# The gated convolution's input projection by seven block products, and block products added up in PSUM

## The chip, the cores and the metric

The kernel runs on one core of a Trainium2 chip. The metric is the device time of one execution in microseconds. Of several executions the median is given, with the lowest and the highest. PE is the matmul engine, PEld its weight loads, DVE the vector engine, ACT the scalar (activation) engine, POOL the general one, SP the engine whose queue issues most transfers. PSUM is the memory into which PE writes; it has eight banks of 512 float32 values per partition.

## The reference

The program takes 1024 prompt tokens and 32 sample tokens through two layers of width 1024. Layer 0 has one input projection of 2048 columns: 512 for a pooling mixer (trailing means over 2, 4, 8 and 16 tokens, by groups of 128 channels) and 3 x 512 for a gated short convolution. Cut to that part:

```python
hcat = x @ w_in_even                            # (tokens, 2048)
a_in, b_gate, c_gate, h_in = hcat[..., :512], hcat[..., 512:1024], hcat[..., 1024:1536], hcat[..., 1536:]
ya = pool_mixer(a_in)                           # trailing means minus the token, a map per group
cv = w[0]*ch[t-2] + w[1]*ch[t-1] + w[2]*ch[t]   # ch = c_gate * h_in, causal, three taps
yb = b_gate * cv
mix = concat(ya, yb) @ w_out_even
x = LN(alpha * x + mix)
x = LN(alpha * x + (silu(x @ w1) * (x @ w3)) @ w2)   # SwiGLU, 2816 hidden features
x = x + (ple @ w_ple) * sigmoid(x @ w_gate)
```

Layer 1 has other mixers (spatial gating, a state-space scan) and the same output projection, SwiGLU and embedding. All matrices are float32, and the result has to keep that precision.

## The kernel before, in words

Activations lie on chip with features on partitions: `xh` and `xl` are the operand of all 1056 tokens in two float32r parts whose sum is exact, `stream` is the residual. A weight is loaded (`Weights.raw`, L76), split into two parts in the same way (`Weights.split`, L86: the high part on ACT, the low part on DVE) and kept in a ring of four places of two halves each (`place`, `half`, L63 to L74). `plan` (L147) writes down the order of use; `get` (L135) hands a weight out and prepares those that follow, four halves ahead. A product of weight and operand takes three matmuls: high by high, low by high, high by low.

**Layer 0's mixer** (`layer0_mixer`, L317). The four pooling tiles come first, two at a time (windows 2 and 4, then 8 and 16). `feature_mm` (L232) makes one output tile of 128 features for one chunk of tokens (384, 384, 288): 8 k-tiles by 3 matmuls. ACT copies it out (L352 to L355); DVE makes the window sums (L361) and differences (L368 to L374); a small product maps each group (L380). Then the convolution: four groups of three tiles (c_gate, h_in, b_gate), for each chunk three `feature_mm`, a copy of c_gate on ACT (L392), the product c_gate * h_in (L396), the three taps (L399, L401), and the gate (L407). The results go to `yf`, which is split into the operand of the output projection (L414). PSUM holds six banks "mm" and two "ms".

**The up projection of SwiGLU** (`up`, L829) makes hidden tiles two at a time by Winograd's form of Strassen's algorithm: with the contraction and the pair of tiles cut in halves, and the tokens in halves of 528, seven products of blocks replace eight. `block_sums` (L878) makes the sums T1 to T4 of the operand's blocks, each in two parts. One product (L902) is 4 k-tiles by 3 by two matmuls of 264 columns, 24 in all, into a PSUM tile of two banks; "q" has four such tiles. `quad` (L934) takes the seven products of a pair in the order 1, 6, 7, 5, 2, 3, 4, each in a PSUM tile of its own; one is copied to SBUF by ACT (L937), and DVE adds the others there, seven additions (L922). Then come silu on ACT (L930) or the multiplication with silu's result on DVE (L932). There are nine such rounds of two pairs (w1, w3) in each layer, behind a first pair in an order of its own. During the last pair the first loads of the down projection go out (`load`, L1039), each behind the product that is the last to read the memory they overwrite.

The order of the instructions of each engine is fixed when the program is built: from those whose operands are ready by its own reckoning the builder takes the one that stands first in the program, so an instruction can come ahead of earlier ones that still wait. A tile of memory is handed out again when all its readers are done; a new pool's tiles wait for those of closed pools whose memory they take. On the chip each engine takes its queue in that fixed order.

```python
def quad(self, key, dst, gate, last=False):                    # L934
    nc.scalar.activation(self.block(dst, 0, 0), self.product(key, 1), AF.Copy)
    self.add(dst, (0, 1), self.product(key, 6), (0, 0))
    ...
    self.add(dst, (1, 0), self.product(key, 4))
    self.act(dst, gate)
```

Of the kernel before, what the change touches and what calls it, by code (L numbers as in the profile page):

```python
# [14 lines left out]
P = 128  # L15
# [16 lines left out]
# Matmul time, in us, from a chunk's last product to its statistics' matmuls, on to their broadcast, and  # L32
# between the pieces of what is normalised.
# [17 lines left out]


class Weights:
    """What the matmuls take beside the operand kept on chip, in the order of its use: loaded, then split
    exactly, w = hi + lo, into two float32r parts, AHEAD half places ahead of the matmuls."""
# [3 lines left out]
    def __init__(self, nc, pool, order):  # L59
        self.nc, self.pool, self.count, self.rest = nc, pool, 0, None  # L60
        self.made, self.items, self.temps = [], self._make(order), None
# [20 lines left out]
    def temp(self, n):  # L82
        self.count += 1
        return self.temps.tile([P, TH], F32, tag="bf", name=f"bf{self.count}", bufs=5)[:, :n]
# [12 lines left out]
    def _make(self, order):  # L97
        for kind, key, src in order:
# [7 lines left out]
            else:  # L106
                # The blocks of two hidden tiles' weights, and Winograd's sums of them.
                r0, r1 = (self.raw(v) for v in src)
                a11, a12, a21, a22 = (r[:, h * 512:(h + 1) * 512] for r in (r0, r1) for h in range(2))
                own = lambda x: (key, 1, self.split(self.half(), x))  # noqa: E731  # L110
                if kind != "sums":
                    yield own(a11)
                if kind == "own":
# [3 lines left out]
                if kind != "own":  # L117
                    yield own(s2)
                    yield own(self.sub(a11, a21))
                    yield own(s1)  # L120
                if kind == "all":
                    yield own(a12)
                if kind != "sums":
                    yield own(self.sub(a12, s2))
                if kind == "all":
                    yield own(a22)
# [20 lines left out]
def plan(a, steps, ple):  # L147
    """The order in which the weights are used."""
# [6 lines left out]
    for layer in range(2):  # L155
        if layer == 0:
            add("w_in0", *range(16))
# [24 lines left out]
class Later(list):  # L182
    """Chunks of an operand, whose last pieces may be still to come from deferred steps."""
# [11 lines left out]
class Kernel:  # L195
# [16 lines left out]
    def passed(self, columns):  # L212
        """Account for matmul columns issued; run the steps that are due."""
# [5 lines left out]
    def mm3(self, ps, w, sel, x, k, lo, n, first, last):  # L219
        """ps += W_k^T x_k with both operands in two exact parts."""  # L220
# [11 lines left out]
    def feature_mm(self, w, x, c, kk=KD, sel=None, k0=0):  # L232
        """One output tile [128 features, tokens of chunk c]."""
# [12 lines left out]
    def build(self):  # L246
        nc, tc, a = self.nc, self.tc, self.a
        with ExitStack() as ctx:
# [7 lines left out]
            self.stream = const.tile([P, KD, T], F32, name="stream")  # L256
            self.acc = [self.stream[:, :, t0:t0 + n] for t0, n in CH]
# [4 lines left out]
            nc.sync.dma_start(out=self.acc[0][:, 0:2, :], in_=xin[:, 0:2, t0:t0 + n])  # L262
            self.w.prefetch()
            for c, (t0, n) in enumerate(CH):
                for k in range(0 if c else 2, KD, 2):
                    nc.sync.dma_start(out=self.acc[c][:, k:k + 2, :], in_=xin[:, k:k + 2, t0:t0 + n])
# [16 lines left out]
            for c in range(3):  # L283
                for k in range(0, KD, 2):
                    self.split(self.x[c], slice(k, k + 2), self.acc[c][:, k:k + 2, :])
# [3 lines left out]
            # The hidden tiles, [parity, token half, pair, tokens of the half].  # L289
            self.hidden = [dram.tile([P, 2, 2, NG, TH], F32, name=f"hidden{i}") for i in range(2)]  # L290
            for layer in range(2):
                (self.layer1_mixer if layer else self.layer0_mixer)(self.x)
                with ExitStack() as stack:
                    self.hp = stack.enter_context(tc.tile_pool(name=f"h{layer}", bufs=1, reuse_waits="tile"))
                    self.w.temps = self.hp
# [14 lines left out]
    def split(self, x, ks, src):  # L310
        """x = hi + lo, exactly, for k-tiles ks of some tokens."""
# [5 lines left out]
    def layer0_mixer(self, x):  # L317
        nc, tc, a = self.nc, self.tc, self.a
        W = 15 + SEQ + 15 + DEC
        with ExitStack() as ctx:  # L320
            mp = ctx.enter_context(tc.tile_pool(name="mix0", bufs=1, reuse_waits="tile"))
# [3 lines left out]
            self.psum_bufs = {"mm": 6, "ms": 2}  # L325
# [4 lines left out]
            yf = [mp.tile([P, KD, CH[c][1]], F32, tag=f"yf{c}", name=f"yf{c}") for c in range(3)]  # L330

            # Products of zeros bring the tensor engine's clock up while the first loads come.
            zeros = yf[0][:, 0, :]
            nc.vector.memset(zeros, 0.0)
            ps = self.bank("ms")
            for _ in range(WARM):
                nc.tensor.matmul(ps[:, :CH[0][1]], zeros[:, :P], zeros, start=True, stop=True)

            ds = []
            for g0 in (0, 2):  # L340
                units = self.w.get(("w_in0", g0), ("w_in0", g0 + 1))
                us = []
# [1170 lines left out]
```

## Time and profile before

| what | value |
|---|---|
| three runs | 2346.04, 2354.27, 2354.75 us; median 2354.27 |
| profiled execution | span 2343.1 us from its first to its last instruction; no time besides its span is listed |
| mean granted clock of PE | 0.998 of 2.4 GHz |
| PE busy | 2322.3 us, 99% of the span |
| DVE busy | 1580.9 us, 67% |
| ACT busy | 905.2 us, 39% |
| moved by DMA | 203 MB, 87 GB/s on average |

Busy time of PE counts pipelined matmuls, so its durations (0.28 us for a matmul of 264 columns) overlap; the distance between the starts of two matmuls is what one costs. A wait is put down to the instruction that ended last before it. The stages lie like this: pooling to 58.5 us, the convolution to 202 us, output projection, norm and the first two hidden tiles to some 350 us, the up projection from there to 762 us, the down projection behind it; layer 1 fills the second half.

### The profile page before, as it was taken

How to read it: one execution, taken by the hardware profiler on the slowest of the kernel's cores; microseconds unless marked ns; L12 is line 12 of the kernel's file. 1: busy time of each engine (PE TensorE's matmuls, PEld its weight loads, DVE VectorE, ACT ScalarE, POOL GpSimd, SP SyncE). 2: the span in 40 equal slices, each digit the busy share in tenths (PEclk: the TensorE clock that was granted, in tenths of full speed). 3: DMA queues.
4: the chain of work that ended last, by engine and by line, in shares of the span. 5: the costliest groups of instructions: out<-in, count | busy, mean ns of one | idle time of the engine just before them, and what ended most of it. 6: DMA issues, size and time to landing. Idle time of an engine off the chain costs nothing.

```text
span 2343.1 us, 40948 instructions
## 1 busy us (share of the span) xinstructions
PE 2322.3 (99%) x17423; PEld 2289.4 (98%) x17423; DVE 1580.9 (67%) x2494; ACT 905.2 (39%) x1501; POOL 71.2 (3%) x88
## 2 busy tenths in 40 slices
PE   9999999999999999999999999999999999999998
PEld 8999999999999999999999989999999999999998
DVE  4434698666666878776655774788666665978773
ACT  4212254323232443464542662354232222434462
POOL 0000010000000000010000120100000000000100
PEclk9999999999999999999999999999999999999999
DMA  4110113222224622024211322122222225611132
GB/s 156 47 55 28 42 59 110 73 92 73 79 82 137 247 78 69 28 82 140 88 47 40 109 64 79 37 73 101 79 84 67 88 68 199 227 60 47 40 100 92
DMA packets 81289, 203.03 MB, mean 87 GB/s; under 512 B 10220, under 2 KB 16564, under 8 KB 81108
## 3 DMA queue, kind: packets, MB, share of 16 engines
q1 hardware_dynamic: 80340, 199.74, 25.8%
q8 instruction: 137, 2.24, 0.4%
q10 hardware_dynamic: 768, 0.68, 0.1%
q14 instruction: 44, 0.36, 0.0%
HBM read 167.24 MB, written 33.16 MB: 86 GB/s over the span
## 4 chain that ended last, share of the span: by engine, by line
PE 93%; DVE 3%; DMA 1%; POOL 1%; ACT 1%; issue 0%; SPq 0%; POOLq 0%; ACTq 0%
PE q L910 32%; PE q L1108 20%; PE mm L224 8%; PE mm L225 8%; PE mm L226 8%; PE q L1236 8%; PE q L1215 2%; PE mm L568 1%; PE mm L569 1%; PE mm L570 1%; DVE bf L94 1%; DMA raw<-w 1%; PE ms L704 1%; DVE w L89 0%; PE q L1317 0%
## 5 line engine op out<-in xcount | busy, mean ns | idle before, releaser
L1108 PE MATMUL q<-w 128*128 128x264 f32 x3696 | 458.3, 286 | 0.0
L1108 PEld LDWEIGHTS q<-w 128*128 128x128 f32 x3696 | 457.3, 189 | 0.0
L88 ACT ACTIVATE w<-raw 128x512 fp32r<-128x512 f32 (+2 forms) x240 | 189.6, 799 | 288.8 <-PE mm L226 107.6
L89 DVE TENSOR_TENSOR w<-raw,w 128x512 fp32r<-128x512 f32 (+2 forms) x240 | 218.3, 911 | 56.9 <-ACT w L88 56.1
L88 ACT ACTIVATE w<-bf 128x512 fp32r<-128x512 f32 (+1 forms) x226 | 138.3, 631 | 303.0 <-PE q L910 132.6
L224 PE MATMUL mm<-xhin,w 128*128 128x384 f32 (+1 forms) x672 | 219.2, 327 | 2.6 <-ACT w L88 1.5
L226 PE MATMUL mm<-xlin,w 128*128 128x384 f32 (+1 forms) x672 | 217.4, 325 | 0.0
L225 PE MATMUL mm<-xhin,w 128*128 128x384 f32 (+1 forms) x672 | 217.1, 324 | 0.0
L910 PE MATMUL q<-xhgate,w 128*128 128x264 f32 x1280 | 207.9, 284 | 1.4 <-ACT xhgate L884 0.8
L910 PE MATMUL q<-xhin,w 128*128 128x264 f32 x1280 | 208.0, 284 | 0.7 <-DVE c L815 0.6
L224 PE MATMUL mm<-xhgate,w 128*128 128x384 f32 (+1 forms) x576 | 188.2, 327 | 1.1 <-ACT xhgate L313 1.1
L226 PE MATMUL mm<-xlgate,w 128*128 128x384 f32 (+1 forms) x576 | 186.7, 325 | 0.0
L225 PE MATMUL mm<-xhgate,w 128*128 128x384 f32 (+1 forms) x576 | 186.6, 325 | 0.0
L910 PEld LDWEIGHTS q<-xhgate,w 128*128 128x128 f32 x1280 | 177.0, 188 | 1.8 <-ACT xhgate L884 1.0
L910 PEld LDWEIGHTS q<-xhin,w 128*128 128x128 f32 x1280 | 177.0, 188 | 1.1 <-issue 0.8
L89 DVE TENSOR_TENSOR w<-bf,w 128x512 fp32r<-128x512 f32 (+1 forms) x226 | 152.0, 690 | 23.4 <-ACT w L88 22.2
L1236 PE MATMUL q<-xhgate,w 128*128 128x264 f32 x1024 | 166.7, 285 | 0.0
L922 DVE TENSOR_TENSOR c<-c,q 128x528 f32<-128x528 f32 x142 | 98.0, 702 | 99.5 <-PE q L910 99.4
L922 DVE TENSOR_TENSOR s<-s,q 128x528 f32<-128x528 f32 x142 | 97.7, 701 | 78.5 <-PE q L910 78.1
L1236 PEld LDWEIGHTS q<-xhgate,w 128*128 128x128 f32 x1024 | 141.6, 188 | 0.0
L224 PEld LDWEIGHTS mm<-xhin,w 128*128 128x128 f32 x672 | 126.4, 188 | 4.7 <-ACT w L88 2.3
L910 PE MATMUL q<-xlgate,w 128*128 128x264 f32 x640 | 130.0, 284 | 0.4 <-DVE xlgate L885 0.4
(301 smaller groups left out, 4286.8 us busy)
## 6 DMA issues: line engine op xcount, KB each, us to landing
raw<-w SPq DMA_DIRECT2D x116, 512.0 KB, 3.6
hidden<-c SPq DMA_DIRECT2D x44, 528.0 KB, 3.9
raw<-w_gate SPq DMA_DIRECT2D x32, 512.0 KB, 3.6
raw<-w_in SPq DMA_DIRECT2D x16, 512.0 KB, 3.6
raw<-w_out SPq DMA_DIRECT2D x16, 512.0 KB, 3.6
xhdown<-hidden SPq DMA_DIRECT2D x12, 528.0 KB, 9.0
t2down<-hidden SPq DMA_DIRECT2D x8, 528.0 KB, 3.9
t3down<-hidden SPq DMA_DIRECT2D x8, 528.0 KB, 4.9
```

The source lines that it names most:

```text
L88: self.nc.scalar.activation(hi, x, AF.Copy)
L89: self.nc.vector.tensor_tensor(lo, x, hi.bitcast(F32), op=ALU.subtract)
L94: self.nc.vector.tensor_tensor(t, a, b, op=op)
L224: nc.tensor.matmul(ps, wh, xh, start=first, stop=False)
L225: nc.tensor.matmul(ps, wl, xh, start=False, stop=False)
L226: nc.tensor.matmul(ps, wh, xl, start=False, stop=last)
L568: nc.tensor.matmul(o, xh, hi[:, s], start=k == 0, stop=False)
L910: nc.tensor.matmul(ps[:, a, :TH // 2], w[q][:, ks], x[r][:, k, a * TH // 2:(a + 1) * TH // 2], start=k == 0 and j == 0, stop=k == 3 and j ...
L922: self.nc.vector.tensor_tensor(self.block(dst, *at), self.block(dst, *(to or at)), ps, op=ALU.add)
L1108: nc.tensor.matmul(ps[m][:, a, :TH // 2], v[q][:, ms], x[r][:, a * TH // 2:(a + 1) * TH // 2], start=j == 0 and n == 0, stop=j == NG - 1 a ...
L1215: nc.tensor.matmul(ps[:, b, :TH // 2], w[q][:, o:o + P], pe[k][r][:, t * TH + b * TH // 2:t * TH + (b + 1) * TH // 2], start=k == 0 and i ...
L1236: nc.tensor.matmul(ps[:, b, :TH // 2], w[q][:, ks], token_half((self.xh, self.xl), k, t, b)[r], start=k == 0 and i == 0, stop=k == KD - 1 ...
```

## The change

The twelve tiles of the convolution are made in six pairs by the seven products (c_gate, h_in and b_gate of tiles 0 and 1, then of 2 and 3). For this the mixer makes T1, T2, T3 from the raw input in the pooling stage, and T4 at the start of the convolution, over part of the operand. T1 and T2 lie in the memory of `stream`, so the raw input goes to a tile of the mixer instead, and the residual is loaded again during and behind the last pair (`residual`). The pooling groups change places: windows 8 and 16 first. The taps run over all 1056 tokens at once.

`quad` takes the products in the order 1, 2, 6, 5, 7, 3, 4, in both layers' up projection too. Products 6, 7 and 4 are added by PE to the PSUM tile of product 1, product 3 to that of product 5; between them ACT copies the running sum to the blocks where it belongs, and DVE adds only products that are wanted elsewhere. `plan` and `_make` follow that order. The rest of the diff takes comments away.

```diff
-            add("w_in0", *range(16))
+            add("w_in0", 2, 3, 0, 1)
+            for i in (0, 2):
+                for j in range(3):
+                    order.append(("all", ("conv", j, i), [a["w_in0"][4 + 3 * (i + k) + j] for k in range(2)]))
...
+        xraw = self.mp.tile([P, KD, T], F32, tag="yf", name="xraw")
...
+    def residual(self, c):
+        t0, n = CH[c]
+        self.nc.sync.dma_start(out=self.acc[c], in_=self.a["xT"][:, :, t0:t0 + n])
...
+            self.psum_bufs = {"ms": 2, "mm": 6, "q": 3}
+            self.w.temps, self.w.temp_bufs = mp, 3
+            t3 = mp.tile([P, 8, TH], F32R, name="t3mix")
+            t12 = self.const.tile([P, 16, TH], F32R, tag="stream", name="t12mix", bufs=1)
...
+    def pooling(self, stack, x, xraw, wg, pool_out, sums):
+        pp = stack.enter_context(tc.tile_pool(name="pooling", bufs=1, reuse_waits="tile"))
...
+        for g0 in (2, 0):
+            units = self.w.get(("w_in0", g0), ("w_in0", g0 + 1))
+            if yf is None:
+                self.block_sums(xraw, *sums)
...
+    def gated_conv(self, stack, conv_out, t2, t4, b21):
+        cp = stack.enter_context(tc.tile_pool(name="conv0", bufs=1, reuse_waits="tile"))
...
+        d = cp.tile([P, 4, TH], F32, tag="chp", name="t4mix", bufs=1)
+        sub(d, b21[0].bitcast(F32), t2[0].bitcast(F32))
+        sub(d, d, b21[1].bitcast(F32), ALU.add)
+        sub(d, d, t2[1].bitcast(F32))
+        nc.scalar.activation(t4[0], d, AF.Copy)
+        sub(t4[1], d, t4[0].bitcast(F32))
...
+        for i in (0, 2):
+            cs = cp.tile([P, 2, T], F32, tag="cs", name=f"cs{i}", bufs=1)
+            self.quad(("conv", 0, i), cs, None, AF.Copy)
+            chp = cp.tile([P, 2, 4 + T], F32, tag="chp", name=f"chp{i}", bufs=1)
...
+            self.quad(("conv", 1, i), chp[:, :, 2:2 + T], cs)
...
+            cv = cp.tile([P, 2, T], F32, tag="cs", name=f"cv{i}", bufs=1)
...
+            def free(p):
+                if p == 1:
+                    parts((0, 2), slice(0, CH[0][1]))
+                    parts((0, 2), slice(CH[0][1], TH))
+                if p == 2:
+                    parts((4,), slice(0, TH))
+                if p == 5:
+                    self.stream = self.const.tile([P, KD, T], F32, tag="stream", name="stream", bufs=1)
+                    self.acc = [self.stream[:, :, t0:t0 + n] for t0, n in CH]
+                    self.residual(0)
+
+            self.quad(("conv", 2, i), yf[:, 4 + i:6 + i, :], cv, step=free if tail else None)
+        for c in (1, 2):
+            self.residual(c)
...
-        (w,), ps = self.w.get(key), self.quads()
+        (w,), add = self.w.get(key), ps is not None
+        ps = ps if add else self.quads()
...
-                        start=k == 0 and j == 0, stop=k == 3 and j == 2,
+                        start=not add and k == 0 and j == 0, stop=k == 3 and j == 2, skip_group_check=add,
...
+    def quad(self, key, dst, gate, func=None, step=None):
+        def made(i, ps=None):
+            ps = self.product(key, i, ps)
+            if step:
+                step(i)
+            return ps
+
+        u = made(1)
+        self.copy(dst, (0, 0), u)
+        self.add(dst, (0, 0), made(2))
+        self.act(dst, (0, 0), gate, func)
+        made(6, u)
+        self.copy(dst, (0, 1), u)
+        v = made(5)
+        self.copy(dst, (1, 1), v)
+        made(7, u)
+        self.add(dst, (1, 1), u)
+        self.act(dst, (1, 1), gate, func)
+        made(3, v)
+        self.add(dst, (0, 1), v)
+        self.act(dst, (0, 1), gate, func)
+        made(4, u)
+        self.act(dst, (1, 0), gate, func, u)
...
+        def behind(p):
+            for n in {6: (1,), 7: (2, 3)}.get(p, ()):
+                self.load(n)
```

## Rows read from the trace of the kernel before

**Rows 1.** The page's head and its part 1, whole kernel.
```profile
span 2343.1 us, 40948 instructions
...
PE 2322.3 (99%) x17423; PEld 2289.4 (98%) x17423; DVE 1580.9 (67%) x2494; ACT 905.2 (39%) x1501; POOL 71.2 (3%) x88
```

**Rows 2.** Busy time by stretch: pooling (first two), convolution, up projection (last).
```profile
6.50:31.00 24.50, 23.59 (x145) 23.34 (x146) 16.34 (x18) 14.49 (x23) 0.00 (x0) 1.00 0.72 263
31.00:58.50 27.50, 27.50 (x160) 25.41 (x159) 9.24 (x16) 8.43 (x20) 0.00 (x0) 1.00 0.14 40
58.50:202.00 143.50, 143.50 (x879) 141.48 (x878) 58.20 (x91) 37.22 (x66) 0.00 (x0) 1.00 0.15 45
395.00:762.00 367.00, 367.00 (x3021) 367.00 (x3020) 235.57 (x363) 107.73 (x182) 0.00 (x0) 1.00 0.28 92
```

**Rows 3.** Waits of PE, whole kernel: who for whom, total us, times, longest.
```profile
PE mm L224 <- ACT w L88: 1.5, 2, 0.9
...
PE q L910 <- DVE c L815: 1.3, 2, 0.6
```

**Rows 4.** ACT in order of time, convolution: first chunk, second and fourth group of tiles.
```profile
101.65 0.49 ACT L392 ACTIVATE cs<-mm 128x384 f32<-128x384 f32 x1 [3.22 <-PE mm L226]
...
171.26 0.49 ACT L392 ACTIVATE cs<-mm 128x384 f32<-128x384 f32 x1 [3.22 <-PE mm L226]
```

**Rows 5.** One line's instructions, L937, 395 to 900 us: durations, first and last start.
```profile
L937 ACT ACTIVATE s<-q x9: 612/612/616, 398.6 to 725.0; 128x528 f32<-128x528 f32 x9
```

**Rows 6.** PE in order of time, convolution: matmuls of 384 columns, one per line.
```profile
99.81 0.34 PE L224 MATMUL mm<-xhin,w 128*128 128x384 f32 x1
...
101.91 0.34 PE L224 MATMUL mm<-xhin,w 128*128 128x384 f32 x1
```

**Rows 7.** Groups by line, first 500 us: name, shapes, count, busy, mean ns, idle before.
```profile
L89 DVE TENSOR_TENSOR w<-raw,w 128x1024 fp32r<-128x1024 f32 x28 | 34.2, 1223 | 20.9 <-ACT w L88 20.8
...
L922 DVE TENSOR_TENSOR s<-s,q 128x528 f32<-128x528 f32 x29 | 19.9, 701 | 12.8 <-PE q L910 12.7
...
L930 ACT ACTIVATE s<-s 128x528 f32<-128x528 f32 x16 | 10.2, 641 | 11.7 <-DVE s L922 11.3
...
L361 DVE TENSOR_TENSOR s<-u 128x1085 f32<-128x1085 f32 x4 | 5.2, 1288 | 22.1 <-ACT u L355 22.1
```

**Rows 8.** DVE in order of time: second pooling pair, first and last operation.
```profile
55.84 1.29 DVE L361 TENSOR_TENSOR s<-u 128x1085 f32<-128x1085 f32 x1 [18.07 <-ACT u L355]
...
70.42 0.18 DVE L374 TENSOR_TENSOR d<-d,u 128x16 f32<-128x16 f32 x1
```

**Rows 9.** Chain of waits, merged, from 0 to 260 us: pooling's small products on PE.
```profile
64.79 1.47 PE ms L380 x4
66.44 0.60 PE ms L380 x2
```

**Rows 10.** Groups by line, layer 1, 1340 to 1410 us: the widest splits.
```profile
L314 DVE TENSOR_TENSOR xlgate<-u,xhgate 128x1536 fp32r<-128x1536 f32 x2 | 3.5, 1754 | 0.0
...
L313 ACT ACTIVATE xhgate<-u 128x1536 fp32r<-128x1536 f32 x2 | 3.0, 1478 | 0.0
```

**Rows 11.** Busy time by stretch: DMA at its densest, from 10 to 20 us.
```profile
10.00:20.00 10.00, 10.00 (x59) 10.00 (x58) 8.08 (x10) 6.96 (x11) 0.00 (x0) 1.00 1.07 396
```

**Rows 12.** DMA issues: KB each, median us from issue to landing.
```profile
raw<-w_out SPq DMA_DIRECT2D x16, 512.0 KB, 3.6
...
stream<-spill SPq DMA_DIRECT2D x2, 1536.0 KB, 8.9
```

**Rows 13.** SP, then PE in order of time: the down projection's first loads and product.
```profile
748.41 0.38 SPq L1014 DMA_DIRECT2D t2down<-hidden  x1
...
762.73 7.54 PE L1108 MATMUL q<-w 128*128 128x264 f32 x60
```

**Rows 14.** Waits of ACT and DVE, up projection, layer 0: total us, times, longest.
```profile
ACT w L88 <- DVE bf L94: 34.4, 17, 4.8
...
DVE bf L94 <- DMA raw<-w: 38.6, 15, 4.2
```

More of the change, by code (lines that the diff above doesn't have):

```diff
@@ L60, in __init__ @@
         self.nc, self.pool, self.count, self.rest = nc, pool, 0, None
-        self.made, self.items, self.temps = [], self._make(order), None
+        self.made, self.items, self.temps, self.temp_bufs = [], self._make(order), None, 5
     def place(self):
@@ L112, in _make @@
                     yield own(a11)
-                if kind == "own":
                     yield own(a12)
@@ L116, in _make @@
                 s2 = self.sub(s1, a11)
-                if kind != "own":
-                    yield own(s2)
-                    yield own(self.sub(a11, a21))
-                    yield own(s1)
[L121 to L126, printed above, removed]
+                if kind == "own":
+                    yield own(self.sub(a12, s2))
+                    continue
+                yield own(s2)
+                if kind == "all":
+                    yield own(s1)
+                yield own(self.sub(a11, a21))
+                if kind == "sums":
+                    yield own(s1)
+                    continue
+                yield own(self.sub(a12, s2))
+                yield own(a22)
     def prefetch(self, n=AHEAD):
@@ L408, in layer0_mixer @@
-                nc.scalar.activation(conv_out[:, i, 0:2], chp[:, SEQ:SEQ + 2], AF.Copy)
-                nc.scalar.activation(conv_out[:, i, 2:4], chp[:, 2 + T:4 + T], AF.Copy)
-            nc.scalar.dma_start(out=a["o_conv"], in_=conv_out)
-            for c in range(3):
-                for k in range(0, KD, 2):
-                    self.split(self.x[c], slice(k, k + 2), yf[c][:, k:k + 2, :])
+                            out=out, in0=src[:, m, k:k + n], scalar=w[k], in1=out, op0=ALU.mult, op1=ALU.add
+                        )
@@ L850, in up @@
             for m, t in ((0, 0), (1, 0), (0, 1)):
-                nc.scalar.activation(self.block(dst, m, t), p1, AF.Copy)
+                self.copy(dst, (m, t), p1)
             self.add(dst, (0, 0), self.product((layer, w, 1), 2))
@@ L934, in quad @@
-    def quad(self, key, dst, gate, last=False):
-        nc = self.nc
-        nc.scalar.activation(self.block(dst, 0, 0), self.product(key, 1), AF.Copy)
-        self.add(dst, (0, 1), self.product(key, 6), (0, 0))
-        if last:
-            self.load(1)
-        self.add(dst, (1, 0), self.product(key, 7), (0, 1))
-        if last:
-            self.load(2)
-        p5 = self.product(key, 5)
-        if last:
-            self.load(3)
-        self.add(dst, (0, 1), p5)
-        self.add(dst, (1, 1), p5, (1, 0))
-        self.add(dst, (0, 0), self.product(key, 2))
-        self.add(dst, (0, 1), self.product(key, 3))
-        self.add(dst, (1, 0), self.product(key, 4))
-        self.act(dst, gate)
+    @staticmethod
@@ new lines, in used, with copy, add, act @@
+    def used(ps):
+        return ps[:, :, :TH // 2]
+    def copy(self, dst, at, ps):
+        self.nc.scalar.activation(self.block(dst, *at), self.used(ps), AF.Copy)
+    def add(self, dst, at, ps, src=None):
+        self.nc.vector.tensor_tensor(
+            self.block(dst, *at), self.block(dst, *(src or at)), self.used(ps), op=ALU.add
+        )
+    def act(self, dst, at, gate, func=AF.Silu, ps=None):
+        nc, x = self.nc, self.block(dst, *at)
+        src = x if ps is None else self.used(ps)
+        if gate is not None:
+            nc.vector.tensor_tensor(x, src, self.block(gate, *at), op=ALU.mult)
+        elif ps is not None or func != AF.Copy:
+            nc.scalar.activation(x, src, func)
```

208 lines of the change are left out of this document (109 added, 99 removed).

## The prediction

> **What bounds the kernel now.** The page comes first: PE, the matmul engine, is busy 2322.3 of 2343.1 us [rows 1]. Over the whole span only some 21 us are left in which it does nothing, so hardly any wait can be removed; what makes the kernel shorter is fewer matmul columns. Next the busy time by stretch: in the 143.5 us of the convolution and in 367 us of the up projection PE is busy all the time, at a granted clock of 1.00 (the 2.4 GHz level), while DVE is busy 58 of 143.5 us and 236 of 367 us, ACT less [rows 2]. Both have room, and so what the change takes off DVE in the up projection is worth nothing, and what it adds to DVE in the mixer costs nothing unless PE comes to wait for it. Third the waits of PE: the long stretches have none; what there is sits where stages meet, at 0.6 to 0.9 us [rows 3]. The forecast is then the columns saved, less the new waits at the new meeting points.
>
> The sum is made against the profiled execution, whose span is 2343.1 us; its own time is not listed beside the runs. The shortest of the three runs, 2346.0, lies 2.9 us above that span, the median 11.2 us above it. I take a difference off the median; about 0.5% (11.8 us) is what a measurement of this kernel can tell from no change.
>
> **The matmuls of the convolution.** Before: four groups of three feature tiles. From the first chunk of the second group to that of the fourth pass 171.26 - 101.65 = 69.61 us, or 34.80 a group, 11.60 a tile [rows 4]; twelve tiles are 139.2 us. After: six pairs of tiles by seven products, 42 products of 24 matmuls with 264 columns. The same products run in the up projection: the first ACT copy of every second pair starts 326.4 us after that of eight rounds before [rows 5], a round is two pairs, 14 products, so one product takes 326.4 / 8 / 14 = 2.914 us. 42 of them are 122.4 us. Saved: 16.8 us. That is just the ratio of columns, 7/8: 24 x 1056 x 12 = 304,128 before, 266,112 after, at 0.457 ns a column either way.
>
> A rule bears on this. Twelve matmuls of 384 columns follow one another in 101.91 - 99.81 = 2.10 us, 0.175 each [rows 6], 9% over 384 columns at 2.4 GHz. The Trainium skill, VectorE: DVE Perf Modes, section The TRN2 errata, gives a matmul 6 cycles more than its columns, so 0.1625 us here. By that rule twelve tiles would take 128.9 and 42 products 113.4 us, a saving estimated at 15.5. The trace does not agree on the level; I stay with the rows' 16.8.
>
> **Pooling, in the other order and with block sums.** The products of its four tiles stay. New on DVE are 24 operations for T1, T2, T3 (0.70 us each [rows 7], 16.9 us) and on ACT 12 of 0.64 us. In the pooling stretches DVE is idle 24.5 - 16.3 + 27.5 - 9.2 = 26.5 us, ACT 29 us [rows 2]; so they fit, and nothing of PE waits for them, because the six banks of the second pair hold all six of its outputs. I cost this at nothing; without that cover the pooling sums would end late, which is the next term.
>
> **T4 and the end of pooling.** This is the tightest place. T4 overwrites part of the operand, and its working tile lies in the memory of the pooling tiles, so it begins only when the last pooling matmul has read its input. Before, the second pair's sums on DVE ran from 55.84 to 70.6 us [rows 8], with seven window additions; now windows 2 and 4 come last, with three. Four additions of 1.29 us less [rows 7]: 65.4 us, or about 63 if no weight work is mixed in. Then three small products on PE, 1.47 + 0.60 = 2.1 us [rows 9]: 65.1 to 67.5. Then three DVE operations over 2112 elements, one on ACT, one on DVE. Scaled from 1536 elements (1.754 and 1.478 us [rows 10]) they take 2.41 and 2.03 us, 4 x 2.41 + 2.03 = 11.7 us. T4 is there at 76.8 to 79.2 us. It is wanted by the seventh product of the first pair: 58.5 us, where the stretches of [rows 2] part, two sets of small products (4.2) and six products (17.5), so at 80.2. The slack is 1 to 3 us, and DVE operations for weights, 0.70 us each, can be queued in between: at worst ten, so PE waits 0 to 6 us. I take 1.5, nearer the low end, since T4 stands ahead of the pairs in the program. The first copy of a pair also needs that memory, free at about 65 us; the third product wants it at about 66: 0 to 2 us, taken 0.3.
>
> **Other meeting points.** The first product's PSUM tile lies where pooling's banks lay: the same meeting before cost 0.6 us [rows 3], taken as it is. In the last pair the splits of the pooling output (two of 768 elements, two of 288) stand ahead of the copy of product 1 on ACT, at least 2.0 us by [rows 10], and the third product waits for that copy: 0 to 1.5, taken 0.5. Behind the last pair three loads bring the residual back, 4.3 MB, on SP's queue; they go out when product 5 has read T1, 8.7 us before the end, and two of the four w_out loads may stand behind them. DMA moved 396 GB/s at its densest [rows 11] and 263 over the first stretch [rows 2]: 11 or 16.5 us, so w_out's third unit, loaded in 3.6 us [rows 12] and split in some 2.2 (1.22 on DVE [rows 7], about 1.0 on ACT by [rows 10]), is there 8 to 14 us behind the end, and wanted at 8.4 (four outputs of 12 matmuls, 2.1 us each [rows 6]). 0 to 5 us, taken 0.5, near the low end, since the unit's load can also go out before them. A chunk's residual alone lands in 8.9 us [rows 12], most of it before the end, and six banks of 2.1 us cover the rest.
>
> **The up projection.** Nothing is gained: PE waits nowhere there. Of each pair four additions leave DVE and two copies come to ACT (0.64 us each [rows 7]; ACT is idle 259 of 367 us). The new thing is that PE writes again into a bank that was just copied, with one product between, 2.9 us for a copy of 0.64. Cost nothing, from 0 to the rival below. The down projection's first loads now go behind the third product, not the second: 2.9 us later than the 14.3 us from 748.41 to 762.73 [rows 13]. 11.4 us are still enough for a load of 3.6 [rows 12] and two steps' splits (four of 1.3 us, ACT and DVE together, by [rows 7]); 0 to 2 us, taken 0.
>
> **The sum.** -16.8 + 1.5 + 0.3 + 0.6 + 0.5 + 0.5 = -13.4 us. 2354.3 - 13.4 = 2341 us. With every unknown at its low end it is -16.2, with all at the high end of the mixer -16.8 + 15.1 = -1.7.
>
> **Rivals.** *Late T4 and late loads:* the terms near their high ends together, 8 to 15 us lost. For it: DVE has a full plate from 20 to 80 us, and slacks are 1 to 3 us. Against: the program order puts T4 first. 2346 to 2353.
>
> *No free bank:* the mixer has three PSUM tiles, and a pair's first tile is read until behind its last product. If the next pair got that very tile, PE would wait for an operation of 0.70 us and its handover at each of five pair starts, 0.6 [rows 3] to 0.9 us: 3 to 4.5 us, and the time would be 2344 to 2346. Against: the tile of product 2 is free by then. The Trainium skill, Perfetto Trace Analysis, section Optimizing Tensor Performance, asks for just that rotation of banks between groups; by it the reuse of one bank after a single product speaks against the change. No row here shows which bank is taken.
>
> *The copies come late in the up projection:* the other side. ACT's queue also holds the weights' splits, and these wait for sums that wait for loads: 17 waits, 2.0 us on average and 4.8 at most, behind 15 waits of DVE for loads, of up to 4.2 us [rows 14]. A copy queued behind the longest comes after the 2.3 us that it has to spare, and PE stands. There are 36 such pairs: at 1 us each 36 us, 2377 us. It decides from 13.4 / 36 = 0.37 us a pair. Against: the average wait just fits, and DVE has 5.6 us less to do in a round.
>
> **How the numbers follow.** Forecast 0.62, late T4 and loads 0.18, no free bank 0.10, late copies 0.10. Most of the forecast's own cases (2338 to 2344) gain over 11.8 us, some fall short: faster 0.54, same 0.38, slower 0.08. The range: upwards it takes in the first two rivals, 2352; downwards a median of three may fall on the lower of the two levels that the runs show, 2346.0 - 13.4 = 2333, and with the whole saving 2330.
>
> **What would show it.** Right: six rounds of seven products in the convolution stretch at 2.91 us, that stretch near 130 us for 143.5, PE's waits in it under 4 us, the largest on T4 (line of the last mixer sum) before the seventh product, and no wait of PE in the up projection. Wrong: PE waiting for ACT or DVE at each pair, there or in the mixer; a gap behind the convolution that a w_out split ends; a product longer than 2.92 us.

## The result and the profile after

The changed kernel takes 2332.1 us (median of four runs, 2331.3 to 2334.1), the kernel before 2350.2 (four runs, the three above among them, 2344.5 to 2354.8). The ratio is 0.9935, with a 95% interval from 0.9918 to 0.9951: some 15 us, or 0.65%, faster. (The ratio is made of fast runs alone; that of the two medians is 0.9923, some 18 us.) The spans of the two profiled executions are 2343.1 and 2329.6 us, 13.5 apart; the forecast of the difference was 13.4. Each is one execution: a second profiled execution of both gave spans 10.4 apart (2343.1 and 2332.7).

The head and part 1 of the page after answer to [rows 1]: PE's busy time fell by 15.3 us, a little more than the span, and DVE's by 37.5.

```profile
span 2329.6 us, 41097 instructions
...
PE 2307.0 (99%) x17567; PEld 2273.9 (98%) x17567; DVE 1543.4 (66%) x2426; ACT 966.1 (41%) x1616; POOL 71.4 (3%) x88
```

Busy time by stretch, after: the convolution from its first product to the output projection's first matmul, and 367 us of the up projection. They answer to the last two of [rows 2] (columns as there).

```profile
59.76:186.51 126.75, 126.75 (x1021) 125.16 (x1021) 89.78 (x130) 50.86 (x88) 0.00 (x0) 1.00 0.21 66
383.00:750.00 367.00, 367.00 (x3020) 367.00 (x3020) 187.68 (x292) 126.61 (x218) 0.00 (x0) 1.00 0.27 89
```

PE is still busy all the time in both. The convolution is shorter, with DVE and ACT busier in it; the up projection has 48 us less for DVE and 19 more for ACT, and PE's time is what it was.

Where the 13.5 us come from, by the first starts of each stage's lines in PE's order of time:

| stretch | before | after | difference |
|---|---|---|---|
| start to the convolution's first matmul | 58.30 | 59.76 | +1.46 |
| convolution | 143.29 | 126.75 | -16.54 |
| output projection, norm, first hidden tiles | 151.55 | 153.02 | +1.47 |
| up projection, layer 0 | 409.59 | 410.86 | +1.27 |
| down projection to the second norm's first sums, either layer | 225.16 | 225.16 | 0 |
| second norm to the embedding, layer 0 | 35.07 | 33.56 | -1.51 |
| embedding, and layer 1 to its up projection | 547.09 | 545.60 | -1.49 |
| up projection, layer 1 | 410.30 | 409.54 | -0.76 |
| second norm to the embedding, layer 1 | 33.58 | 36.18 | +2.60 |

The convolution alone gives 16.5 us. The stretch ahead of it and the two behind give 4.2 back. The rows below are small, and have both signs; the traces of both kernels taken again tell which of all these rows repeat.

The waits of PE, whole kernel, answer to [rows 3] (who for whom, total us, times, longest):

```profile
PE mm L228 <- ACT w L88: 1.8, 1, 1.8
...
PE q L990 <- ACT xhin L963: 0.8, 1, 0.8
PE mm L229 <- DVE w L89: 0.6, 1, 0.6
PE q L990 <- DVE xlin L964: 0.6, 2, 0.4
PE q L990 <- ACT u L393: 0.6, 1, 0.6
```

None in the mixer is for a copy of a block product, an addition or T4 (the two on L963 and L964 are in the first pair of the up projection). Where they stand shows in PE in order of time: the start, the convolution's first product, its end, and the output projection's third weight unit.

```profile
9.07 0.45 PE L228 MATMUL mm<-xhin,w 128*128 128x384 f32 x1 [1.81 <-ACT w L88]
...
59.76 0.51 PE L990 MATMUL q<-xhin,w 128*128 128x264 f32 x2 [0.56 <-ACT u L393]
...
186.51 0.34 PE L228 MATMUL mm<-xhin,w 128*128 128x384 f32 x1
...
194.75 0.34 PE L230 MATMUL mm<-xlin,w 128*128 128x384 f32 x1
195.20 0.62 PE L228 MATMUL mm<-xhin,w 128*128 128x384 f32 x2
196.46 0.45 PE L229 MATMUL mm<-xhin,w 128*128 128x384 f32 x1 [0.64 <-DVE w L89]
```

From 194.75 to 196.46 three matmuls take 1.71 us, where 3 x 0.175 would do: PE loses 1.2 us there, of which 0.64 is listed as a wait. Its cause stands on SP and on ACT, in order of time:

```profile
177.92 4.02 SPq L330 DMA_DIRECT2D stream<-xT  x3
182.06 17.42 SPq L79 DMA_DIRECT2D raw<-w_out  x4
```

```profile
194.09 1.06 ACT L88 ACTIVATE w<-raw 128x1024 fp32r<-128x1024 f32 x1 [5.00 <-DMA raw<-w_out]
```

All three loads of the residual were issued before the output projection's third weight unit, which then landed 12 us behind its issue at 182.06, where [rows 12] had 3.6.

### The profile page after: what moved, and what is told of

Read it like the earlier page. It is cut to its first block, busy times and chain, and to the rows that moved or that the text cites. A ratio compares the mean times of both kernels' runs of the same rounds, so it can differ in the third digit from the quotient of the medians.

```text
span 2329.6 us, 41097 instructions
## 1 busy us (share of the span) xinstructions
PE 2307.0 (99%) x17567; PEld 2273.9 (98%) x17567; DVE 1543.4 (66%) x2426; ACT 966.1 (41%) x1616; POOL 71.4 (3%) x88
## 4 chain that ended last, share of the span: by engine, by line
PE 94%; DVE 3%; DMA 1%; POOL 1%; ACT 1%; issue 0%; SPq 0%; POOLq 0%; ACTq 0%
PE q L990 38%; PE q L1203 20%; PE q L1331 8%; PE mm L228 6%; PE mm L229 6%; PE mm L230 6%; PE q L1310 2%; PE mm L639 1%; PE mm L640 1%; PE mm L641 1%; DVE bf L94 1%; PE ms L775 1%; DVE w L89 1%; DMA raw<-w_out 1%; DMA raw<-w 0%
## 5 line engine op out<-in xcount | busy, mean ns | idle before, releaser
L990 PE MATMUL q<-xhin,w 128*128 128x264 f32 x1664 | 270.7, 284 | 2.0 <-ACT xhin L963 0.8
L89 DVE TENSOR_TENSOR w<-raw,w 128x512 fp32r<-128x512 f32 (+2 forms) x246 | 212.8, 878 | 55.1 <-ACT w L88 54.8
L89 DVE TENSOR_TENSOR w<-bf,w 128x512 fp32r<-128x512 f32 (+1 forms) x250 | 167.0, 691 | 106.7 <-ACT w L88 105.5
L990 PEld LDWEIGHTS q<-xhin,w 128*128 128x128 f32 x1664 | 230.1, 188 | 3.0 <-ACT xhin L963 1.0
L88 ACT ACTIVATE w<-bf 128x512 fp32r<-128x512 f32 (+1 forms) x250 | 149.0, 629 | 195.9 <-PE q L990 77.9
L990 PE MATMUL q<-xlin,w 128*128 128x264 f32 x832 | 169.9, 285 | 0.6 <-DVE xlin L964 0.6
L990 PEld LDWEIGHTS q<-xlin,w 128*128 128x128 f32 x832 | 128.8, 188 | 1.3 <-DVE xlin L964 1.0
L228 PE MATMUL mm<-xhin,w 128*128 128x384 f32 (+1 forms) x384 | 125.5, 328 | 3.0 <-ACT w L88 1.8
L229 PE MATMUL mm<-xhin,w 128*128 128x384 f32 (+1 forms) x384 | 124.2, 325 | 0.6 <-DVE w L89 0.6
L94 DVE TENSOR_TENSOR bf<-raw 128x512 f32<-128x512 f32 x50 | 34.5, 691 | 135.8 <-DMA raw<-w 129.8
L230 PE MATMUL mm<-xlin,w 128*128 128x384 f32 (+1 forms) x384 | 123.9, 325 | 0.0
```

The lines of the kernel that those rows point to most:

```text
L88: self.nc.scalar.activation(hi, x, AF.Copy)
L89: self.nc.vector.tensor_tensor(lo, x, hi.bitcast(F32), op=ALU.subtract)
L94: self.nc.vector.tensor_tensor(t, a, b, op=op)
L228: nc.tensor.matmul(ps, wh, xh, start=first, stop=False)
L229: nc.tensor.matmul(ps, wl, xh, start=False, stop=False)
L230: nc.tensor.matmul(ps, wh, xl, start=False, stop=last)
```

## The experiments

The theory: the whole gain is the convolution's columns, less the meeting points at its two ends. The rivals: a part comes from the new order in the up projection; PSUM tiles are waited for; copies come late. For timed kernels the ratio is that to the kernel before on the same chip, with its interval.

**One part alone: the convolution.** The new mixer, with before's order of products in the up projection:

```diff
-            self.quad((layer, 1, g), s, None, AF.Silu)
+            self.old_quad((layer, 1, g), s, None)      # the seven products as before, no accumulation
```

> The convolution by seven products as in the changed kernel, the up projection with the pairs of before (no accumulation into a used bank, eight block additions on DVE). Theory A, the whole gain is the convolution's: the up projection's first product stands where it stands in the changed kernel, about 13.6 us ahead of before, the 367 us of the up projection stay full, and the time is that of the changed kernel, 2332 us, within 3 us. Rival B, part of the gain comes from the new order of products in the up projection (the medians differ by 18 us, the convolution's sum is only 13.6): 2336 to 2338 us. Rival C, the accumulation costs something there that the convolution pays for: below 2329 us.

Measured: 2334.8 us, ratio 0.9949 (0.9936 to 0.9961); the up projection takes 411.1 us in layer 0. Busy time by stretch in it:

```profile
384.00:751.00 367.00, 367.00 (x3022) 367.00 (x3021) 235.29 (x363) 108.28 (x182) 0.00 (x0) 1.00 0.29 92
```

**The other part alone: the up projection.** The mixer of before, the new order behind it:

```diff
-        self.add(dst, (0, 1), self.product(key, 6), (0, 0))
+        made(6, u)
+        self.copy(dst, (0, 1), u)
```

> The kernel before, with the convolution untouched, and the up projection with the new order of products and the accumulation in PSUM. Theory A: the same as before within 0.2%, a ratio of 0.998 to 1.002, PE full through the up projection and no wait of PE there for ACT or DVE; DVE's busy time in the up projection falls from about 236 to about 186 us and buys nothing. Rival B: 4 to 5 us faster, a ratio of 0.998 or less. Rival of the prediction, late copies: at 36 pairs, slower by 36 us for each us of wait, a ratio above 1.005.

Measured: 2345.5 us, ratio 0.9993 (0.9983 to 1.0002); the up projections take 409.9 and 410.4 us, before 409.6 and 410.3.

```profile
395.00:762.00 367.00, 366.92 (x3018) 366.70 (x3017) 187.79 (x293) 126.89 (x219) 0.00 (x0) 1.00 0.27 88
```

The convolution alone keeps most of the gain, and its interval and that of the whole change overlap. The up projection alone gives nothing that can be told from none: 48 us less work for DVE under a full PE bought nothing. By its interval a share of up to 0.17% (4 us) stays possible; the ratio of 0.998 or less of rival B lies outside it, and in the trace both up projections are no shorter than before.

**The loads behind the convolution.**

```diff
-        for c in (1, 2):
-            self.residual(c)                            # at the end of the mixer
                 units = self.w.get(*[(f"w_out{layer}", 4 * g + i) for i in range(4)])
+                if g == 0:
+                    for c in (1, 2):
+                        self.residual(c)
```

> The changed kernel, but the second and third chunk of the residual are loaded behind the output projection's first four weight units, not ahead of two of them. Theory: the third unit's split on ACT, at 194.1 us in the changed kernel, comes 6 us or more sooner, the wait of PE for the split on DVE (L89, 0.6 us, and 1.2 us lost in all) goes, and the up projection's first product comes 1.2 us sooner: 2331 us, a ratio to before some 0.0005 below the changed kernel's 0.9935. The residual's second chunk is wanted 17 us behind the first output and lands in about 9, so nothing new waits. Rival: the late unit is held by its buffer (the second raw buffer comes free at 180.7 us) and not by the residual's loads: then the split stays at 190 us or later and nothing is gained.

Measured: 2330.6 us, ratio 0.9933 (0.992 to 0.9947). From the convolution's end to the up projection's first product it is 151.63 us, 1.39 less than with the change and what it was before (151.55). SP and ACT in order of time:

```profile
177.68 0.65 SPq L330 DMA_DIRECT2D stream<-xT  x1
178.80 2.04 SPq L79 DMA_DIRECT2D raw<-w_out  x2
180.90 3.23 SPq L330 DMA_DIRECT2D stream<-xT  x2
```

```profile
188.74 1.99 ACT L88 ACTIVATE w<-raw 128x1024 fp32r<-128x1024 f32 x2
```

The unit is split 5.4 us sooner and nothing waits for it: the queue it stood in was the cause, not its buffer. The runs cannot tell 2330.6 from 2332.1; the stretch in the trace can.

**No product between the copy and the next matmuls into its bank.**

```diff
-        self.add(dst, (0, 0), made(2))
-        self.act(dst, (0, 0), gate, func)
         made(6, u)
         self.copy(dst, (0, 1), u)
+        self.add(dst, (0, 0), made(2))
+        self.act(dst, (0, 0), gate, func)
```

> The changed kernel, but product 6 adds to the bank of product 1 at once, with no product between them (order 1, 6, 2, 5, 7, 3, 4), in the convolution and in the up projection of both layers: 42 pairs. Theory, the one product between hides the copy and nothing else is slow in writing again into a used bank: now PE waits in each pair for the copy on ACT, 0.61 us, and the handover on both sides, some 0.5 to 0.6: 1.1 to 1.3 us a pair, 46 to 55 us in all, 2378 to 2387 us. Rival, the hardware or the program holds no order between the copy and the matmuls that costs PE, or ACT is so far ahead that it is hidden: 2332 us. Rival, the copies are late behind weight splits on ACT as often as in the prediction's last rival: 2 us a pair and more, above 2410 us.

Measured: 2342.3 us, 10 more than with the change; ratio 0.9984 (0.9966 to 1.0003). The convolution takes 1.4 us more, the up projections 4.9 and 5.1: 11.4 / 42 = 0.27 us a pair, a quarter of what was expected. PE in order of time, second pair of the convolution:

```profile
86.36 0.65 PE L992 MATMUL q<-xhin,w 128*128 128x264 f32 x4
86.85 0.40 PE L992 MATMUL q<-xlin,w 128*128 128x264 f32 x2
87.28 3.16 PE L992 MATMUL q<-t12mix,w 128*128 128x264 f32 x24
90.29 0.65 PE L992 MATMUL q<-xhin,w 128*128 128x264 f32 x4
```

Product 1 began at 83.44 and its 24 matmuls end at about 86.35. The six from 86.36 on are product 2's first, though product 2 stands behind product 6 in the text: the builder laid them in PE's queue ahead of product 6. They take 0.73 us; then 0.19 are left (behind two matmuls from 86.85 the next could start at 87.09), and another 0.11 on the matmul behind the one that waited:

```profile
87.51 2.94 PE L992 MATMUL q<-t12mix,w 128*128 128x264 f32 x23
```

This is the same product 6 from its second matmul on, 0.23 us behind the first in place of 0.12. Leaving product 1 for product 2 (86.36) and coming back to product 2 (90.29) cost nothing. So a copy and its handover want about 0.9 us here, and most of that was filled when the program was built. It is so in the up projection of layer 0 too: 18 matmuls that wait start late by 2.7 us together, those right behind them by another 1.9, which is 4.6 of its 4.9 us.

**The same PSUM tile at every pair start.**

```diff
-        ps = ps if add else self.quads()
+        ps = ps if add else self.quads("qu" if i == 1 and "qu" in self.psum_bufs else "q")   # bufs: qu 1, q 2
```

> The changed kernel, but in the convolution the first product of every pair has one PSUM tile of its own, so that it must take the tile which the last operation of the pair before has just read. Theory: PE waits at each of the five later pair starts for that operation, 0.70 us on DVE (0.61 where it is a copy on ACT), and its handover: 1.1 to 1.3 us each, 5.5 to 6.5 us in all, 2337 to 2339 us; in the changed kernel another tile was taken. Rival, the changed kernel already takes that very tile, and the wait is hidden by the order of the operations: no wait, 2332 us.

Measured: 2331.8 us (one run); the convolution takes 127.58 us, 0.8 more than with the change, and no wait is listed. PE in order of time where the second pair begins:

```profile
83.78 0.40 PE L990 MATMUL q<-xlin,w 128*128 128x264 f32 x2
84.16 0.75 PE L990 MATMUL q<-xhin,w 128*128 128x264 f32 x4
```

The same again: in PE's queue as built, six to eight matmuls of product 2 stand ahead of product 1, and 0.14 us is what is seen of the tile's reuse (84.16 less 84.02), with another 0.11 on the matmul behind. At the five pair starts these come to 0.8 us.

**Two PSUM tiles in place of three.** `"q": 3` becomes `"q": 2` in the mixer.

> The changed kernel, with two PSUM tiles for the block products of the convolution in place of three. Theory: each tile is free again one product (2.9 us) before it is wanted, behind a copy or an addition of 0.6 to 0.7 us, and where it isn't, the queue of PE is built with the next product's matmuls moved ahead; PE's order is almost that of the changed kernel: no wait at the pair starts, the convolution takes 126.75 us as there, 2332 us in all. Rival, no free bank: 3 to 6 us more in the convolution, five pair starts of 0.6 to 1.2 us.

Measured: 2329.4 us (one run); the convolution takes 128.22 us, 1.5 more. PE in order of time:

```profile
174.46 2.71 PE L990 MATMUL q<-t3mix,w 128*128 128x264 f32 x20 [0.70 <-ACT yf L1006]
...
180.80 0.39 PE L990 MATMUL q<-xhin,w 128*128 128x264 f32 x1 [0.21 <-ACT yf L1006]
```

No wait at a pair start. The two that came are in the last pair, where the splits of the pooling output hold ACT ahead of the copies: the place that the prediction named, though three tiles cover all but 0.15 us of it. The time is shorter none the less, since the convolution began 1.2 us sooner, the weight unit behind it was in time, and the up projection of layer 0 took 409.5 us. (Beside it, on its chip, the kernel before took 2342.6 us, one run; whole times from different chips say little about 2 or 3 us.)

**Pooling in the old order.** `for g0 in (2, 0)` becomes `(0, 2)`, and the weights' order with it.

> The changed kernel, with the pooling tiles in the order of before (windows 2 and 4 first, 8 and 16 last), so that seven window additions and not three stand ahead of T4. Theory, T4 is ready less than 1 us ahead of its use in the changed kernel (its last operation ends at 80.5 us, the seventh product starts at 81.3): four additions of 1.29 us make it 5.2 us late, less 0.7: PE waits 4 to 5 us for it at the end of the first pair, and up to 5 us at the first copies or small products, which stand behind the same additions, in place of and not beside it; 2336 to 2338 us. Rival, DVE has slack between the additions and T4, which the trace of the changed kernel does not show: no wait, 2332 us.

Measured: 2339.3 us (one run); the convolution takes 134.20 us, 7.45 more. PE in order of time:

```profile
72.90 2.88 PE L421 MATMUL ms<-d,wg 128*128 128x384 f32 x6 [2.90 <-DVE d L414]
76.87 5.01 PE L990 MATMUL q<-t12mix,w 128*128 128x264 f32 x24 [1.09 <-ACT cs L1006]
...
81.72 0.65 PE L990 MATMUL q<-xhin,w 128*128 128x264 f32 x4
```

Busy time by stretch from the second of these waits on (the third column from the end is the granted clock):

```profile
76.87:81.00 4.13, 4.13 (x19) 4.13 (x20) 4.13 (x3) 0.45 (x1) 0.00 (x0) 0.50 0.00 0
81.00:85.00 4.00, 4.00 (x33) 3.82 (x32) 1.98 (x3) 1.65 (x3) 0.00 (x0) 1.00 0.00 0
```

The waits are as large as expected, 2.90 and 1.09 us, in the second of the places named: PE waits for the last pooling sum, then for the first copy, whose memory comes free behind it. T4 itself is never waited for. The loss is larger because the clock fell behind the waits: the 24 matmuls of product 6 take 4.85 us (76.87 to 81.72), where 2.91 would do, at a granted clock of 0.50, the level of 1.2 GHz. So some 1.9 of the 7.45 us went in that product at the lower clock, and the rest, beside the 4.0 of listed waits, stands in small products that follow one another more slowly and in starts behind a wait. In this one execution the order of the pooling tiles is worth 7 us; how much of the clock's share repeats was not tried.

**Copies made slow.**

```diff
-        self.nc.scalar.activation(self.block(dst, *at), self.used(ps), AF.Copy)
+        for _ in range(4 if self.psum_bufs["q"] == 4 else 1):        # 8 in the second kernel
+            self.nc.scalar.activation(self.block(dst, *at), self.used(ps), AF.Copy)
```

> The changed kernel, with every copy from PSUM in the up projection done four times over on ACT (the copies of the first pair too). Theory: with one product between, a copy has 2.9 us; four take 0.61 + 3 x 0.51 = 2.1 us and the handover some 0.4, so nothing waits: the up projection (its first product to the down projection's first) stays at 411 us in layer 0 and 410 in layer 1, 2332 us in all. Rival, late copies: ACT's queue holds weight splits that wait for loads; a third of the 108 meetings late by 1 us each is 36 us more.

> The same with eight copies in place of one: 0.61 + 7 x 0.51 = 4.2 us and 0.4, some 1.7 us beyond the one product that lies between. Theory A, PE's queue is in the order of the program's text: 3 such meetings in each of 36 pairs, up to 180 us more. Theory B, the queue is built with other products' matmuls moved ahead of the late one: most of it is covered, under 60 us more, though ACT is then busy 320 of 367 us in the up projection and the weight splits behind the copies can come late too.

Measured, one run each: 2348.9 and 2427.1 us, 17 and 95 more. From the up projection's first product to the second norm's first sums the two layers take 11.0 and 8.6 us more with four copies, 44.3 and 52.5 with eight. The first line of PE's waits, with four and with eight:

```profile
PE q L990 <- ACT s L1007: 4.2, 6, 1.5
```

```profile
PE q L990 <- ACT s L1007: 57.4, 38, 9.4
```

(The kernel before took 2342.6 us on their chip, one run; the stages of the traces are the safer comparison.) Both numbers missed. Four copies should have been free, and cost 17 us, of which 4.2 are listed as waits. Read matmul by matmul, layer 0's up projection has from 385 us on 29 matmuls that wait for a semaphore and start late, by 7.8 us together, and the matmul right behind each is another 0.10 to 0.11 late, 3.1 in all; the changed kernel has no such gap there. The 63 places where PE changes products without a wait cost nothing (0.04 us at most). Why the copies are late stands on ACT, in order of time:

```profile
407.61 0.61 ACT L1007 ACTIVATE c<-q 128x528 f32<-128x528 f32 x1 [0.73 <-PE q L990]
408.11 0.62 ACT L88 ACTIVATE w<-raw 128x512 fp32r<-128x512 f32 x1
...
409.64 1.26 ACT L1007 ACTIVATE c<-q 128x528 f32<-128x528 f32 x2
```

Weight splits stand between the four copies, which take 3.3 us here (407.61 to 410.90) and not 2.1; product 6 starts at 410.95. Eight cost half of what theory A gives and more than theory B allowed; part of that is clock (a mean granted clock of 0.991, against 0.998 with the change). So the rival of late copies is real; it starts somewhere between one and four copies, and one copy is on the safe side of it.

**Both kernels again.**

> The changed kernel once more, to see which terms repeat from one execution to the next. Theory: the convolution (126.75 us from its first product to the output projection's first) and the 1.2 us lost behind it repeat to 0.1 us; the wait for the second weight unit at the start (1.81 us) changes by up to 1 us, since it ends with a DMA transfer; the up projection's first pair in layer 0 again waits 0.8 us for ACT's split; the stretches around the norms of layers 0 and 1 change by 1 to 3 us where the granted clock falls. Rival: the differences of 1 to 3 us between the traces behind the up projection's start come from the change and repeat.

> The kernel before once more. Theory: from its first to its last feature matmul of the convolution as in the first trace, 143.4 us; the up projections 409.6 and 410.3 us within 1 us; the stretches around the norms differ by 1 to 3 us where the granted clock falls, and where they fall is not the same as in the first trace. Rival: they repeat, and the stretch from the first statistics of the first token half to the embedding in layer 0 takes 35.1 us again and that of layer 1 33.6 us.

Measured: 2334.5 us with the change, 2345.2 before. The convolution took 126.73 us again. Busy time by stretch around the second norm of layer 0, then layer 1 (the last columns are the granted clock, DMA share and GB/s): before and before again,

```profile
987.90:1023.00 35.10, 33.24 (x253) 32.43 (x253) 26.89 (x30) 23.50 (x35) 6.43 (x6) 0.95 0.20 61
2205.50:2239.10 33.60, 31.74 (x253) 30.92 (x253) 26.91 (x30) 23.36 (x35) 6.50 (x6) 1.00 0.20 64
```

```profile
987.80:1021.40 33.60, 31.74 (x253) 30.93 (x253) 26.90 (x30) 23.38 (x35) 6.43 (x6) 1.00 0.20 63
2204.10:2239.10 35.00, 33.32 (x253) 32.49 (x253) 26.93 (x30) 23.49 (x35) 6.50 (x6) 0.95 0.19 61
```

and with the change,

```profile
975.50:1009.10 33.60, 31.73 (x252) 30.88 (x252) 26.94 (x30) 23.34 (x35) 6.45 (x6) 1.00 0.20 63
2189.40:2225.60 36.20, 34.45 (x253) 33.67 (x253) 26.91 (x30) 23.36 (x35) 6.50 (x6) 0.91 0.19 59
```

The same stretch takes 33.6 us at a granted clock of 1.00 and 35.1 or 36.2 at 0.95 or 0.91, with the same instructions, and in which layer it happens changes from one execution to the next. PE waits 1.0 and 0.6 us for POOL in each of them, whether the clock falls or not. So the +2.60 and -1.51 of the table are no part of the change. Nor is the -1.49: the repeats took 547.5 and 547.3 us in that stretch. The -0.76 came back as -0.49.

Nor is most of the +1.46 at the start. The wait for the second weight unit, 1.81 us with the change, is between 0.88 and 1.94 in the ten traces with the new mixer, five of them at 1.08 or less, and 0.86, 0.87 and 1.21 in the three without. Where the load was issued at the same time, 1.80 us, it landed at 7.94 with the change and at 6.72 with two tiles.

Not so the 1.27 us in the up projection of layer 0. It came back as 3.22 (with a granted clock of 0.89 over 15 us of it), and as 1.4 to 1.5 in the kernels with the mixer alone, the loads moved, and one tile for pair starts; with two tiles and with the old pooling order it is gone. DVE in order of time shows where it begins: a weight of the first pair that lands later. With the change, and with two tiles:

```profile
359.71 0.69 DVE L94 TENSOR_TENSOR bf<-raw 128x512 f32<-128x512 f32 x1 [2.74 <-DMA raw<-w]
```

```profile
357.18 0.69 DVE L94 TENSOR_TENSOR bf<-raw 128x512 f32<-128x512 f32 x1 [1.51 <-DMA raw<-w]
```

Before it was 1.41. SP's instructions start at the same distance from the first product until the loads themselves; why the transfer then takes 1.2 us longer in some builds and not in others stays open.

## Why the prediction was right, point by point

**The matmuls: right, -16.8 against -16.5.** Products follow one another at 2.92 us, and the 4.1 to 4.4 us beyond the products' own time are pooling's small products in both kernels. (The prediction calls this just the ratio of columns; 7/8 of its 139.2 us would save 17.4, and the 16.8 come from the two measured spacings, 0.458 and 0.460 ns a column.) The rule of the Trainium skill (VectorE: DVE Perf Modes, The TRN2 errata) gave 15.5; the trace does not agree, neither in the level nor in the saving.

**The block sums: nothing, as costed.** DVE's busy time from 6.5 to 58.5 us went from 25.6 to 47.9 us and no PE wait ends on them.

**T4: too dear, and for the wrong reason.** Its last operation and the seventh product's start, DVE and PE in order of time:

```profile
78.12 2.36 DVE L432 TENSOR_TENSOR xlin<-t4mix,xhin 128x2112 fp32r<-128x2112 f32 x1 [1.83 <-ACT xhin L436]
```

```profile
81.27 0.70 PE L990 MATMUL q<-xhin,w 128*128 128x264 f32 x4
```

It was ready at 80.5, later than the 76.8 to 79.2 of the prediction, and wanted at 81.3: 0.8 us to spare, no wait, where 1.5 was taken and the largest wait of the mixer was looked for. The old pooling order shows what is really tight: the small products and the first copy, at 0.3 in the sum, take the whole of a delay before T4 feels any of it.

**The first copy, the bank, the last pair's splits.** 0 for 0.3, 0.56 for 0.6, 0.15 for 0.5.

**The residual's loads: the mechanism right, the size off.** The term was 0.5, "near the low end, since the unit's load can also go out before them". It did not in this build: the third unit was split at 196.4, 9.9 us behind the convolution's end, inside the 8 to 14 of the prediction and behind the 8.4 at which it was wanted. It cost 1.2 to 1.4, and moving the loads gave that back. A gap behind the convolution that a w_out split ends was one of the prediction's signs of being wrong, and it is there; it is small beside the 16.5.

**What the sum lacked.** Two meeting points: the second weight unit at the start, 1.81 us of wait for 0.86, and the first pair of the up projection, 1.27. Neither was looked at, since the change was not thought to touch them; of the first the traces do not show that it does. In this pair of traces they cost 0.95 and 1.27, about as much as the three terms that came out at or near 0 had taken (1.5, 0.3 and 0.5). That the sum of 13.4 met 13.5 to the tenth is therefore luck: the first four rows of the table alone give 12.3, and the second pair of traces is 10.4 apart.

**The rivals.** No free bank: not there, and even a tile forced to be the same costs 0.8 us in six pairs. The Trainium skill (Perfetto Trace Analysis, Optimizing Tensor Performance) asks independent groups to change banks so that copying one out overlaps the next one's matmuls. The prediction read it as speaking against the new order, which goes too far: the product in another tile that lies between gives that overlap. The traces agree with the rule so far as they go: reuse behind one product of 2.9 us costs nothing that the trace shows, and reuse at once 0.27 us a pair. Late copies: not at one copy. Late T4 and loads: the loads only.

**The level.** 2341 was set off the median of three runs, 2354.3. Beside the first three experiments the kernel before ran seventeen times, 2341.6 to 2351.7, median 2348.7: two of the three runs lay above that whole spread. Much of it goes with the clock: the four runs at a mean granted clock of 0.999 took 2341.6 to 2343.6 us, the five at 0.998 2344.9 to 2349.2, the eight at 0.997 or 0.996 2348.7 to 2351.7. The gain is no clock: three of the four runs with the change were at 0.997, and took 2332.0 to 2334.1.

## What to carry to other kernels

Where one engine is full, price a change by that engine's work alone: 7/8 of the columns gave close to 7/8 of the time, and 48 us less on a neighbour gave nothing. Then list the loads at both ends of the changed stage in queue order, with when each is wanted; loads that were wanted late and issued early cost 1.2 to 1.4 us here, and moving them was two lines. When a cost is argued from the order of the text, look at the engine's order as it was built: three of these experiments came out cheaper than expected because other matmuls had been moved into the gap.

## What the runs showed of the hardware that was not expected

A wait of PE costs more than the profile lists. A matmul of 264 columns counts as busy for 0.28 us and the next starts 0.12 behind it, so a start that is up to 0.16 us late is listed as no wait; and the matmul right behind the late one is late by another 0.10 to 0.11 (29 of 29 in layer 0's up projection with four copies, 18 of 18 without the product between). Both are only seen in the distance between starts. Changing from one product to another without a wait costs nothing.

A short wait can also cost clock, or not. In the repeat, behind 1.60 us of wait at the start, matmuls of 384 columns followed each other at 0.32 us, not 0.175: the granted clock is 0.51 from 8.59 to 11.00 us, the lower of PE's two levels, 1.2 GHz for 2.4. In the first trace with the change a wait of 1.81 us at the same place cost no clock (9.53 to 9.70, 0.17 us from start to start). The old pooling order above lost some 1.9 us in the same way.

```profile
8.59 0.68 PE L228 MATMUL mm<-xhin,w 128*128 128x384 f32 x1 [1.60 <-ACT w L88]
9.07 0.52 PE L229 MATMUL mm<-xhin,w 128*128 128x384 f32 x1
9.39 0.52 PE L230 MATMUL mm<-xlin,w 128*128 128x384 f32 x1
```
